# Block 1's front stage: TensorE's order written out by a plan of threads, and a row-by-row inverse

## The chip, the cores and the metric
One core of one Trainium2 chip runs the whole program; the metric is device microseconds of that core from one launch, as the median of several runs (the lower the better). TensorE (PE) is fed by VectorE (DVE), ScalarE (ACT), and by DMAs that are all issued from the queue of SyncE (SP).

## The reference, cut to what matters
A sequence of 512 tokens of width 1024 passes through two blocks of two layers each. Block 1, which the change touches, computes in each layer:

```
h = rmsnorm(x);  p = h @ w_in                 # 1792 + 1536 + 1024 + 3*1024 columns
y_rw  = rwkv7(p_rw)      # S_t = S_{t-1}(diag(w_t) - kk_t^T (a_t kk_t)) + v_t^T k_t ; y_t = S_t r_t, then group norm, gate
y_ret = retention(p_ret) # rotary, 4 heads, decayed causal scores, rms norm, silu gate
y_sg  = sgu(p_sg)        # gelu, layer norm, causal 128-token mixing
x = x + sum_n(sigmoid(gate_n) * (y_n @ w_branch_n)) @ w_out
x = x + conv_ffn(rmsnorm(x))
```

Block 2 (five attention branches, merge) follows; the change leaves its code alone.

## The kernel before, in words
Activations lie transposed, 128 channels by 512 tokens to a tile. A product with a weight is made of two rounded halves on each side (hi and lo): `mm3` (lines 110 to 112) issues three matmuls for each block of 128 by 128 weights. One `wraw` load of 512 KB holds eight such blocks; ScalarE rounds it to `whi` (L101) and VectorE takes the rest to `wlo` (L102). An output tile of 128 channels (`fm_tile`) is thus 24 matmuls of 512 columns into one PSUM bank of the pool `pm`, which VectorE empties (`evac`, L360, or `gate`, L783). `tm_group` makes a tile with tokens on the partitions, 4 x 24 matmuls of 256 columns. These are called dense work below.

A layer of block 1 has a front stage (everything up to the first `pbr` matmul), a merge (`pbr`, then `w_out`) and a feed-forward part. The front stage holds:

- `rwkv_in`: 14 dense tiles; after tiles 2 to 4, 5 to 7, 8 to 10, 11 to 13 one "pair" of heads is prepared (decays, normalised keys, `psA`). Its two sums over a head (`psk`, `psbon`) go through DRAM and back to be spread over the partitions (`sums`, L137: tiles `sums`, `sumd`, then the target).
- `rwkv_inverse`: 32 triangular 32x32 matrices at once on VectorE: for each of 31 rows one multiply (L487) and one reduction (L489).
- `rwkv_out`: 16 units (4 pairs x 4 chunks of 128 tokens) of small fp32 matmuls that depend on one another (`pst`, `psam`, `psv`, `psg`, `psh`, `psu`, `psy`, `psx`), two units side by side by `robin`, and for each pair `rw_final` (six `psz` steps in a row, `psY`, then a mean and a norm by the same way through DRAM: L642, L650, and the gate).
- `retention`, `sgu` and `gates`: a generator `fill` that `paced` advances by fixed rates (`PACE`) between the steps above. Of the 24 gate tiles 20 are made here and stored to DRAM, 4 are made during the merge (the tuple `e1`).

The order in which each engine gets its instructions is not the order of the code: a scheduler that simulates the engines picks it, by priorities; the code gives evacuations and weight halves a head start of 3000 places (`AHEAD`). Each engine then takes its instructions strictly in that order, so that one that waits holds all that stand behind it. PSUM's eight banks in block 1 are shared out as 3 `pm`, 3 `pw` (chains), 2 `pf` (retention, sgu).

Of the kernel before, what the change touches and what calls it, by code (L numbers as in the profile page):

```python
# [44 lines left out]
HALF = object()  # L45


class Kern:
    BANKS = dict(act=(3, 3, 2), act2=(3, 5, 0))
    AHEAD = 3000  # L50
    PACE = {"in": 0.55, "inv": 3.8, "out": 0.088}
    BUFS = dict(F=8, T=4, h=16, C4=3, Y=8, KR=4, K=4, B=4, V=4, R=2, E=2, WK=7, M=4)
# [258 lines left out]

    def tm_group(self, src, evac):

        ws = [self.weights(src[i], 1024) for i in range(2)]
        for g in range(4):
            ps = self.PM([128, 512])
            for k in range(KD):
                w = ws[k // 4]
# [4 lines left out]
        yield


    def block1_layer(self, l, next_gain, gain1=None, side=None):
# [7 lines left out]
        self.yret, self.ysg = [], []  # L334
        fill = itertools.chain(self.retention(l, win), self.sgu(l, win), self.gates(I["w_gt1"][l], 3, self.cfg.get("e1", (1, 3, 2, 3, 3, 3, 3, 2))))
        self.pump = lambda n: [next(fill, None) for _ in range(n)]
        self.due = 0.0
        self.rwkv_in(l, win)
        self.rwkv_inverse()
        self.paced("inv")  # L340
        yrw = self.rwkv_out(l)
        self.pump(1000)
        ys = [yrw, [self.split(y, *self.seat1(i)) for i, y in enumerate(self.yret)],
              [self.split(y, *self.seat1(4 + i)) for i, y in enumerate(self.ysg)]]
# [5 lines left out]
    def paced(self, part):  # L350

        self.due += self.cfg.get("pace", self.PACE)[part]
        while self.due >= 1:
            self.due -= 1
            self.pump(1)

    def evac(self, ps, tag, name="ev"):
        t = self.tile(tag, name=name)
        with self.tc.high_priority(offset=self.AHEAD):
            self.nc.vector.tensor_tensor(t, ps, self.rb, op=OP.mult)  # L360
        return t


    def rw_mix(self, i, ws, tag):
        nc = self.nc
        p = self.evac(self.fm_tile(ws), "E")
# [3 lines left out]
        self.paced("in")  # L370
        return m

    def rwkv_in(self, l, win):
# [19 lines left out]
        for f in range(4):
            fs = slice(f * 128, (f + 1) * 128)
            r = self.rw_mix(2 + 3 * f, ws, "R")
            k = self.rw_mix(3 + 3 * f, ws, "K")
            vt = self.rw_mix(4 + 3 * f, ws, "V")
            psw = self.P(name="psw")
            nc.tensor.matmul(psw, lhsT=lora[0:64, fs], rhs=m[0:64, :], start=True, stop=True)
            psa = self.P(name="psa")  # L400
            nc.tensor.matmul(psa, lhsT=lora[64:128, fs], rhs=m[64:128, :], start=True, stop=True)
            sw = W("sw")
            nc.scalar.activation(sw, psw, AF.Tanh, bias=half[:, f:f + 1], scale=0.5)
            nc.vector.tensor_scalar(sw, sw, 0.5, 0.5, op0=OP.mult, op1=OP.add)
            a = W("a")
            nc.scalar.activation(a, psa, AF.Tanh, bias=half[:, 4 + f:5 + f], scale=0.5)

            sq = W("sqk")
            nc.scalar.activation(sq, k, AF.Square, scale=v(V_KK + f))

            def inverse(t, ps):
                nc.vector.tensor_scalar(t, ps, 1e-24, None, op0=OP.max)
                nc.scalar.activation(t, t, AF.Sqrt)
                nc.vector.reciprocal(t, t)
            self.sums(sq, self.sel[:, 0], 2, self.P([128, 128], "psk"), sq, inverse)
            kkr = self.tile("B", name="kkr")
# [2 lines left out]
            sc = W("sc")
            nc.vector.tensor_tensor_scan(sc, self.reset, sw, initial=0.0, op0=OP.mult, op1=OP.add)  # L420
            s3 = sc.rearrange("p (c t) -> p c t", t=64)
            dd = self.ap.tile([128, 24], F32, name="dd", tag="dd", bufs=2)
            mid = dd[:, 8:16]
            nc.vector.tensor_copy(mid, s3[:, :, 31])
            nc.vector.tensor_tensor(dd[:, 0:7], s3[:, 0:7, 63], mid[:, 0:7], op=OP.subtract)
            nc.vector.tensor_tensor(dd[:, 0:7], dd[:, 0:7], mid[:, 1:8], op=OP.add)
            nc.scalar.activation(dd[:, 0:7], dd[:, 0:7], AF.Exp, scale=-KAPPA)
            ds = self.ap.tile([128, 8], F32, name="ds", tag="ds", bufs=4)
            nc.sync.dma_start(ds[64:128, 0:7], dd[0:64, 0:7])
            nc.sync.dma_start(ds[0:64, 0:7], dd[64:128, 0:7])  # L430
            self.DD.append(ds)
            nc.vector.tensor_tensor(s3, s3, mid.unsqueeze(2).to_broadcast([128, 8, 64]), op=OP.subtract)
            e1 = W("e1")
            nc.scalar.activation(e1, sc, AF.Exp, scale=-KAPPA)
            nc.vector.tensor_tensor(sw, sc, sw, op=OP.subtract)
            e0 = sw
            nc.scalar.activation(e0, e0, AF.Exp, scale=-KAPPA)
            ei = sc
            nc.scalar.activation(ei, sc, AF.Exp, scale=KAPPA)
            kr = self.tile("KR", (128, 4, 2, 128), name="kr")  # L440
            g4 = lambda t: t.rearrange("p (g t) -> p g t", g=4)
            nc.vector.tensor_tensor(kr[:, :, 0, :], g4(kkr), g4(e0), op=OP.mult)
            nc.vector.tensor_tensor(kr[:, :, 1, :], g4(r), g4(e1), op=OP.mult)
            bd = kkr
            nc.vector.scalar_tensor_tensor(bd, a, 1.0, kkr, op0=OP.add, op1=OP.mult)
            nc.vector.scalar_tensor_tensor(bd, bd, 0.5, ei, op0=OP.mult, op1=OP.mult)

            for e in range(2):
                ps = self.P([128, 4, 64], "psA")
                hs = slice(64 * e, 64 * e + 64)  # L450
                for g in range(4):
                    for c in range(2):
                        cs = slice(64 * c, 64 * c + 64)
                        nc.tensor.matmul(ps[cs, g, :], lhsT=bd[hs, g * 128 + 64 * c:g * 128 + 64 * c + 64],
                                         rhs=kr[hs, g, 0, cs], start=True, stop=True, skip_group_check=True)
                u0 = f * 8 + e * 4
                for b in range(4):
                    bs, ts = slice(32 * b, 32 * b + 32), slice(32 * (b % 2), 32 * (b % 2) + 32)
                    nc.scalar.activation(self.CP[bs, :, u0:u0 + 4].rearrange("p t u -> p u t"), ps[bs, :, ts], AF.Copy)

            nc.vector.tensor_scalar(a, a, -1.0, half[:, 8 + f:9 + f], op0=OP.add, op1=OP.mult)
            nc.vector.scalar_tensor_tensor(k, a, 1.0, k, op0=OP.add, op1=OP.mult)
            nc.vector.scalar_tensor_tensor(r, r, v(V_RK + f), k, op0=OP.mult, op1=OP.mult)
            kd = k
            nc.vector.tensor_tensor(kd, k, ei, op=OP.mult)
            bv = W("bv")
            self.sums(r, self.sel[:, 0], 2, self.P([128, 128], "psbon"), bv,
                      lambda t, ps: nc.scalar.activation(t, ps, AF.Copy))
# [1476 lines left out]
```

## Time and profile before

| | us |
|---|---|
| median of 3 runs (3474.56 to 3478.92) | 3475.21 |
| the profiled execution | 3473.58 |
| its span, first to last instruction | 3471.9 |
| front stage, layer 0: 21.5 to 562.9 | 541.4 |
| merge up to the last `pbr`, layer 0: to 651.8 | 88.9 |
| front stage, layer 1: 1068.7 to 1606.6 | 537.9 |
| merge up to the last `pbr`, layer 1: to 1695.4 | 88.8 |

A front stage is taken from the end of the norm that comes ahead of it (`psb`) to the first `pbr` matmul. In the profile a row's "busy" is the time in which the engine had an instruction in hand; matmuls overlap, so the pace of TensorE is the distance from one start to the next. The granted clock is a share of 2.4 GHz.

### The profile page before, as it was taken

How to read it: one execution, taken by the hardware profiler on the slowest of the kernel's cores; microseconds unless marked ns; L12 is line 12 of the kernel's file. 1: busy time of each engine (PE TensorE's matmuls, PEld its weight loads, DVE VectorE, ACT ScalarE, POOL GpSimd, SP SyncE). 2: the span in 40 equal slices, each digit the busy share in tenths (PEclk: the TensorE clock that was granted, in tenths of full speed). 3: DMA queues.
4: the chain of work that ended last, by engine and by line, in shares of the span. 5: the costliest groups of instructions: out<-in, count | busy, mean ns of one | idle time of the engine just before them, and what ended most of it. 6: DMA issues, size and time to landing. Idle time of an engine off the chain costs nothing.

```text
span 3471.9 us, 47315 instructions
## 1 busy us (share of the span) xinstructions
PE 3332.2 (96%) x17944; PEld 2633.0 (76%) x17944; DVE 2239.1 (64%) x4112; ACT 1346.2 (39%) x2392; POOL 116.2 (3%) x137
## 2 busy tenths in 40 slices
PE   8888999999999989999999999899999999999998
PEld 6667767888887667777888888786778887777776
DVE  5577554687634567564677635797766659866665
ACT  4343223344424433223444434335334443443342
POOL 0000000000000000000000000001001200000031
PEclk9999999999999989999999999999999999999999
DMA  4332224433333331224533335544436554543463
GB/s 137 90 93 62 65 72 155 162 115 97 121 116 99 94 90 52 76 68 153 166 101 95 121 127 156 174 148 124 128 113 230 195 152 135 149 127 120 136 216 137
DMA packets 197940, 431.21 MB, mean 124 GB/s; under 512 B 29512, under 2 KB 57544, under 8 KB 197712
## 3 DMA queue, kind: packets, MB, share of 16 engines
q1 hardware_dynamic: 197712, 428.18, 39.9%
q8 instruction: 142, 2.33, 0.3%
q14 instruction: 86, 0.70, 0.1%
HBM read 337.47 MB, written 59.39 MB: 114 GB/s over the span
## 4 chain that ended last, share of the span: by engine, by line
PE 80%; DMA 9%; DVE 7%; ACT 2%; issue 2%; SPq 1%; POOL 0%; DVEq 0%; ACTq 0%; POOLq 0%
PE pm L112 20%; PE pm L110 19%; PE pm L111 19%; PE pbr L110 2%; PE pbr L112 2%; PE pbr L111 2%; PE psy L1028 2%; DMA sqr<-sumd 2%; PE pspt L1018 2%; DVE wlo L102 1%; DMA sumd<-sums 1%; DMA cc<-sumd 1%; DMA bv<-sumd 1%; DMA sqk<-sumd 1%; PE psl L1000 1%
## 5 line engine op out<-in xcount | busy, mean ns | idle before, releaser
L110 PE MATMUL pm<-shi,whi 128*128 128x512 f32 x3072 | 1230.5, 401 | 10.9 <-ACT whi L101 10.8
L112 PE MATMUL pm<-shi,wlo 128*128 128x512 f32 x3072 | 1221.9, 398 | 3.3 <-DVE wlo L102 3.0
L111 PE MATMUL pm<-slo,whi 128*128 128x512 f32 x3072 | 1221.4, 398 | 0.0
L101 ACT ACTIVATE whi<-wraw 128x1024 fp32r<-128x1024 f32 x480 | 508.5, 1059 | 988.5 <-PE pm L111 671.9
L102 DVE TENSOR_TENSOR wlo<-wraw,whi 128x1024 fp32r<-128x1024 f32 x480 | 588.8, 1227 | 215.6 <-ACT whi L101 208.1
L110 PEld LDWEIGHTS pm<-shi,whi 128*128 128x128 f32 x3072 | 581.7, 189 | 146.1 <-ACT whi L101 16.0
L112 PEld LDWEIGHTS pm<-shi,wlo 128*128 128x128 f32 x3072 | 581.7, 189 | 139.1 <-DVE wlo L102 10.3
L111 PEld LDWEIGHTS pm<-slo,whi 128*128 128x128 f32 x3072 | 582.5, 190 | 125.5 <-issue 10.4
L783 DVE TENSOR_TENSOR gate<-pm,rb 128x512 f32<-128x512 f32 x128 | 88.2, 689 | 196.5 <-PE pm L112 195.9
L360 DVE TENSOR_TENSOR ev<-pm,rb 128x512 f32<-128x512 f32 x140 | 96.2, 688 | 119.1 <-PE pm L112 117.3
L110 PE MATMUL pm<-whi,shi 128*128 128x256 f32 x384 | 115.8, 303 | 3.4 <-ACT whi L101 2.0
L111 PE MATMUL pm<-wlo,shi 128*128 128x256 f32 x384 | 116.0, 302 | 1.5 <-DVE wlo L102 1.4
L112 PE MATMUL pm<-whi,slo 128*128 128x256 f32 x384 | 115.6, 302 | 0.0
L110 PE MATMUL pbr<-shi,whi 128*128 128x512 f32 x288 | 114.2, 397 | 1.4 <-DVE gate L815 1.2
L112 PE MATMUL pbr<-shi,wlo 128*128 128x512 f32 x288 | 113.5, 394 | 0.4 <-DVE wlo L102 0.4
L111 PE MATMUL pbr<-slo,whi 128*128 128x512 f32 x288 | 113.0, 392 | 0.0
L815 DVE SCALAR_TENSOR_TENSOR gate<-gate,pbr 128x512 f32<-128x512 f32 x128 | 85.8, 683 | 33.2 <-PE pbr L112 29.0
L819 POOL TENSOR_TENSOR gate<-gate 128x512 f32<-128x512 f32 x48 | 77.5, 1614 | 606.5 <-DVE gate L815 342.9
L812 ACT ACTIVATE gate<-gate 128x512 f32<-128x512 f32 x128 | 76.4, 624 | 29.4 <-DMA gate<-gtd 28.6
L985 ACT ACTIVATE p<-psl,st 128x256 f32<-128x256 f32 (+3 forms) x128 | 65.1, 513 | 52.2 <-DVE st L983 44.4
L110 PEld LDWEIGHTS pm<-whi,shi 128*128 128x128 f32 x384 | 78.5, 205 | 8.9 <-issue 4.0
L111 PEld LDWEIGHTS pm<-wlo,shi 128*128 128x128 f32 x384 | 78.8, 205 | 8.3 <-issue 5.3
(478 smaller groups left out, 4507.5 us busy)
## 6 DMA issues: line engine op xcount, KB each, us to landing
wraw<-in_w_gt SPq DMA_DIRECT2D x148, 512.0 KB, 3.6
wraw<-in_w_in SPq DMA_DIRECT2D x116, 512.0 KB, 3.7
wraw<-in_f_up SPq DMA_DIRECT2D x88, 512.0 KB, 3.5
gtd<-gate SPq DMA_DIRECT2D x108, 256.0 KB, 2.0
gate<-gtd SPq DMA_DIRECT2D x108, 256.0 KB, 4.1
wraw<-in_w_br SPq DMA_DIRECT2D x44, 512.0 KB, 3.5
wraw<-in_f_dn SPq DMA_DIRECT2D x44, 512.0 KB, 3.5
wraw<-in_w_out SPq DMA_DIRECT2D x32, 512.0 KB, 3.5
```

Of the source, the lines that this page charges most:

```text
L101: nc.scalar.activation(hi[:, :n], raw[:, :n], AF.Copy)
L102: nc.vector.tensor_tensor(lo[:, :n], raw[:, :n], hi[:, :n].bitcast(F32), op=OP.subtract)
L110: nc.tensor.matmul(ps, lhsT=lhs[0], rhs=rhs[0], start=first, stop=False, skip_group_check=skip)
L111: nc.tensor.matmul(ps, lhsT=lhs[0], rhs=rhs[1], start=False, stop=False, skip_group_check=skip)
L112: nc.tensor.matmul(ps, lhsT=lhs[1], rhs=rhs[0], start=False, stop=last, skip_group_check=skip)
L360: self.nc.vector.tensor_tensor(t, ps, self.rb, op=OP.mult)
L783: self.nc.vector.tensor_tensor(t, ps, self.rb, op=OP.mult)
L812: nc.scalar.activation(g, g, AF.Tanh, scale=0.5)
L815: nc.vector.scalar_tensor_tensor(g, g, 1.0, pb, op0=OP.add, op1=OP.mult)
L819: (nc.gpsimd if self.pre and n in self.cfg.get("pa", (1, 2, 3)) else nc.vector).tensor_tensor(g, g, acc, op=OP.add)
L1018: nc.tensor.transpose(pt_[:, b * 128:(b + 1) * 128], ps[e][:, b * 128:(b + 1) * 128], self.ident)
L1028: nc.tensor.matmul(psy[64 * e:64 * e + 64, :], lhsT=vs[e][b], rhs=pts[e][:, b * 128:(b + 1) * 128], start=first and b == 0, stop=last and ...
```

## The change: what it does
The front stage of block 1 is written as generators that yield `Step(cost, wait, chain, inner)`, and a `Plan` walks them: it keeps a time `t` of TensorE's work, takes every chain step that is due, and otherwise a dense piece of the thread of lowest rank (`rwkv_in` 1, retention and sgu 2, gates 3). A dense tile is cut in pieces of two weight blocks (`MORE`), between which due chain steps go; a tile that is begun is finished before another. The plan runs under `manual_schedule(engines={PE})`: TensorE gets its instructions in the order in which the plan traced them; the other engines are ordered by the scheduler as before.

With it come: pairs, units (two lanes), finals, retention's ends as chain threads with declared waits; `late()`, by which a VectorE operation that waits for a DMA is queued behind the evacuation traced last; all 24 gates made in the front stage; the branches in the merge in the order retention, sgu, rwkv (`ORDER1`, with the weights laid out to match); banks 2/4/2; the inverse column by column (outer products: multiply and add of (31-s) x (s+1) elements, s from 1 to 30); v in a zero-padded tile `vp`, copied by ScalarE, so that the second `psy` matmul covers 128 columns; `zs` folded into `cc`; the last gate's `psg` copied by ScalarE.

```diff
+class Plan:
+    def step(self, th):
+        s = next(th["gen"], None)
...
+        self.t += s.cost
+        th["chain"], th["due"] = s.chain, self.t + s.wait
...
+    def run(self):
+        while self.threads:
+            due = sorted((th for th in self.threads if th["chain"] and th["due"] <= self.t), key=lambda th: th["due"])
+            for th in due:
+                self.step(th)
+            dense = [th for th in self.threads if not th["chain"] and th["due"] <= self.t]
+            if self.held:
+                self.step(self.held)
+            elif dense:
+                self.step(min(dense, key=lambda th: th["rank"]))
+            elif self.threads and not due:
+                t = min(th["due"] for th in self.threads)
+                self.lost += max(t - self.t, 0.0)
+                self.t = max(t, self.t)
...
-    BANKS = dict(act=(3, 3, 2), act2=(3, 5, 0))
+    BANKS = dict(act=(2, 4, 2), act2=(3, 5, 0))
...
+        with self.tc.manual_schedule(engines={mybir.EngineType.PE}):
+            plan.add(self.rwkv_in(l, win), 1)
+            plan.add(self.branches(l, win), 2)
+            plan.add(self.gates1(I["w_gt1"][l], 3, (3,) * KD), 3)
+            plan.run()
...
+    def late(self):
+        return self.tc.issue_after(self.last.ins)
...
+        self.sums(sq, self.sel[:, 0], 2, self.P([128, 128], "psk"), sq, inverse)
...
+        yield Chain(0.4, 13.0)
+        kkr = self.tile("B", name="kkr")
+        with self.late():
             nc.vector.scalar_tensor_tensor(kkr, k, v(V_KK + f), sq, op0=OP.mult, op1=OP.mult)
...
-        for t in range(1, 32):
-            nc.vector.tensor_tensor(tmp[:, 0:t, 0:t], R[:, 0:t, 0:t].rearrange("p s c -> p c s"),
-                                    X[:, t, None, 0:t].to_broadcast([128, t, t]), op=OP.mult)
-            nc.vector.tensor_reduce(R[:, t, 0:t], tmp[:, 0:t, 0:t], axis=AX.X, op=OP.add)
+        nc.vector.tensor_copy(R[:, 1:32, 0:1], X[:, 1:32, 0:1])
+        for s in range(1, 31):
+            n, m = 31 - s, s + 1
+            nc.vector.tensor_tensor(tmp[:, 0:n, 0:m], X[:, s + 1:32, s:s + 1].to_broadcast([128, n, m]),
+                                    R[:, s, None, 0:m].to_broadcast([128, n, m]), op=OP.mult)
+            nc.vector.tensor_tensor(R[:, s + 1:32, 0:m], R[:, s + 1:32, 0:m], tmp[:, 0:n, 0:m], op=OP.add)
...
+        vp = self.vp[lane]
+        nc.scalar.activation(vp[:, 0:4:3, :], pst[:, 3, :].rearrange("p (e v) -> p e v", e=2), AF.Copy)
...
-            nc.tensor.matmul(psy[vs, e, :], lhsT=tk[:, 2, vs], rhs=ams[e][:, 384:512],
-                             start=False, stop=True, skip_group_check=True)
+            nc.tensor.matmul(psy[:, e, :], lhsT=vp[:, 2 * e:2 * e + 2, :].rearrange("p a v -> p (a v)"),
+                             rhs=ams[e][:, 384:512], start=False, stop=True)
...
-        yield
-        nc.vector.tensor_tensor(y0, y0, mean, op=OP.add)
-        yield
+        yield Chain(0.4, 10.0)
+        with self.late():
+            nc.vector.tensor_tensor(y0, y0, mean, op=OP.add)
```

## Rows read from the trace of the kernel before

**Rows 1.** The page's head and part 1: span; busy us (share) and instructions.
```profile
span 3471.9 us, 47315 instructions
PE 3332.2 (96%) x17944; PEld 2633.0 (76%) x17944; DVE 2239.1 (64%) x4112; ACT 1346.2 (39%) x2392; POOL 116.2 (3%) x137
```

**Rows 2.** Windows: us, busy (instructions) of each engine, granted clock, DMA share, GB/s.
```profile
21.50:562.90 541.40, 491.96 (x3152) 371.96 (x3151) 324.34 (x596) 182.59 (x374) 0.64 (x1) 0.94 0.28 83
562.90:651.80 88.90, 88.90 (x385) 72.13 (x384) 52.71 (x66) 35.97 (x48) 0.00 (x0) 1.00 0.49 157
1068.70:1606.60 537.90, 495.54 (x3173) 375.51 (x3172) 324.74 (x592) 182.24 (x374) 0.64 (x1) 0.95 0.28 84
...
2650.40:2740.60 90.20, 89.29 (x385) 71.65 (x384) 61.66 (x76) 39.16 (x57) 36.92 (x23) 1.00 0.56 184
```

**Rows 3.** Windows inside layer 0's front stage.
```profile
100.00:200.00 100.00, 83.80 (x444) 59.08 (x443) 58.60 (x94) 43.65 (x69) 0.00 (x0) 0.91 0.34 89
200.00:300.00 100.00, 85.86 (x485) 66.68 (x484) 73.40 (x126) 31.22 (x54) 0.64 (x1) 0.88 0.30 78
```

**Rows 4.** Windows of the instructions on tile pm alone, both front stages.
```profile
21.50:562.90 541.40, 342.04 (x1443) 250.73 (x1443) 30.88 (x45) 7.32 (x16) 0.94 0.28 83
1068.70:1606.60 537.90, 344.41 (x1463) 253.19 (x1463) 30.99 (x45) 7.29 (x16) 0.95 0.28 84
```

**Rows 5.** Timeline of TensorE: start, us, line, operation; dense matmuls at full clock.
```profile
555.20 0.39 PE L112 MATMUL pm<-shi,wlo 128*128 128x512 f32 x1
...
562.68 0.39 PE L112 MATMUL pm<-shi,wlo 128*128 128x512 f32 x1
```

**Rows 6.** Timeline of TensorE: psu, psy and psx of one unit.
```profile
309.09 0.72 PE L575 MATMUL psu<-rhs,tt 128*128 128x128 f32 x5
309.65 0.39 PE L753 MATMUL pssg<-wst,vsg 128*128 128x128 f32 x2
309.88 0.46 PE L583 MATMUL psy<-am,uw 128*128 128x128 f32 x2
310.26 0.43 PE L585 MATMUL psy<-am,tk 128*64 128x128 f32 x2
...
311.40 0.33 PE L600 MATMUL psx<-tk,uw 64*64 64x64 f32 x2
```

**Rows 7.** VectorE's waits in layer 0's front stage: us, times, longest.
```profile
DVE yret L714 <- DMA sqr<-sumd: 21.7, 4, 7.5
DVE y L642 <- DMA cc<-sumd: 20.0, 4, 6.9
DVE bv L469 <- DMA bv<-sumd: 15.6, 4, 5.4
DVE kkr L417 <- DMA sqk<-sumd: 13.1, 3, 5.6
```

**Rows 8.** Timelines of VectorE and TensorE around one such wait.
```profile
146.27 0.69 DVE L714 TENSOR_TENSOR yret<-yret,sqr 128x512 f32<-128x512 f32 x1 [7.48 <-DMA sqr<-sumd]
147.49 1.65 PE L707 MATMUL psret<-pret,vret 128*128 128x384 f32 x2 [5.49 <-DVE pret L706]
```

**Rows 9.** The inverse in layer 0's front stage, by lines: busy us, mean ns.
```profile
L487 DVE TENSOR_TENSOR tmp<-R,X 128x1 f32<-128x1 f32 (+30 forms) x31 | 23.5, 757 | 0.5
L489 DVE TENSOR_REDUCE R<-tmp 128x1 f32<-128x1 f32 (+30 forms) x31 | 15.3, 494 | 0.4
```

**Rows 10.** The chain that ended last: a way through DRAM, and two ends of pairs.
```profile
60.71 0.87 DVE sums L414
...
64.36 6.30 DMA sqk<-sumd
...
351.32 0.96 PE psY L633 x28
...
410.12 0.96 PE psY L633 x28
```

**Rows 11.** Timeline of VectorE in the merge: emptying a pbr bank.
```profile
588.00 0.69 DVE L815 SCALAR_TENSOR_TENSOR gate<-gate,pbr 128x512 f32<-128x512 f32 x1 [0.67 <-PE pbr L112]
```

More of the change, by code (lines that the diff above doesn't have):

```diff
@@ L45, with __init__, Chain, Dense @@
 HALF = object()
+LANES = 2
+class Step:
+    def __init__(self, cost, wait=0.0, chain=False, inner=False):
+        self.cost, self.wait, self.chain, self.inner = cost, wait, chain, inner
+def Chain(cost, wait):
+    return Step(cost, wait, chain=True)
+def Dense(cost):
+    return Step(cost)
+MORE = Step(1.4, inner=True)
+TILE = Dense(1.4)
+class Plan:
+    def __init__(self):
+        self.t, self.threads, self.held, self.lost = 0.0, [], None, 0.0
+    def add(self, gen, rank, wait=0.0):
+        self.threads.append(dict(gen=gen, rank=rank, chain=rank == 0, due=self.t + wait))
+    def step(self, th):
+        s = next(th["gen"], None)
+        if s is None:
+            self.threads.remove(th)
+            self.held = None if self.held is th else self.held
+            return
+        self.t += s.cost
+        th["chain"], th["due"] = s.chain, self.t + s.wait
+        if s.inner:
+            self.held = th
+        elif self.held is th:
+            self.held = None
+    def run(self):
[12 more added lines that the diff above has]
+                self.t = max(t, self.t)
 class Kern:
-    BANKS = dict(act=(3, 3, 2), act2=(3, 5, 0))
+    BANKS = dict(act=(2, 4, 2), act2=(3, 5, 0))
     AHEAD = 3000
-    PACE = {"in": 0.55, "inv": 3.8, "out": 0.088}
-    BUFS = dict(F=8, T=4, h=16, C4=3, Y=8, KR=4, K=4, B=4, V=4, R=2, E=2, WK=7, M=4)
+    BUFS = dict(F=8, T=4, h=16, C4=3, Y=8, KR=4, K=4, B=4, V=4, R=2, E=2, WK=8, M=3)
     BUFS2 = dict(A=23, ix=1, V=6, p=6, pt=4, sw=2, Y=4, c=2, cum=2)
@@ L310, in fm_tile, with fm_steps @@
         return ps
+    def fm_steps(self, ws):
+        ps = self.PM(name="pm")
+        for k in range(KD):
+            self.mm3(ps, next(ws), self.h[k], k == 0, k == KD - 1)
+            if k % 2 and k < KD - 1:
+                yield MORE
+        return ps
     def tm_group(self, src, evac):
@@ L332, in block1_layer @@
         win = I["w_in1"]
[L334 to L344, printed above, removed]
+        self.yret, self.ysg, self.yrw = [], [], [None] * 4
+        plan = self.plan = Plan()
+        with self.tc.manual_schedule(engines={mybir.EngineType.PE}):
[3 more added lines that the diff above has]
+            plan.run()
+        ys = [[self.split(y, *self.seat1(i)) for i, y in enumerate(self.yret)],
+              [self.split(y, *self.seat1(4 + i)) for i, y in enumerate(self.ysg)], self.yrw]
         self.merge(l, ys, I["w_br1"], I["w_out1"], lambda c: self.v(V_N2 + c),
@@ L348, in block1_layer, with branches @@
         self.ffn(l, next_gain, gain1, side)
[L350 to L355, printed above, removed]
+    def branches(self, l, win):
+        yield from self.retention(l, win)
+        yield from self.sgu(l, win)
     def evac(self, ps, tag, name="ev"):
@@ L359, in evac @@
         with self.tc.high_priority(offset=self.AHEAD):
-            self.nc.vector.tensor_tensor(t, ps, self.rb, op=OP.mult)
+            self.last = self.nc.vector.tensor_tensor(t, ps, self.rb, op=OP.mult)
         return t
+    def late(self):
+        return self.tc.issue_after(self.last.ins)
     def rw_mix(self, i, ws, tag):
         nc = self.nc
-        p = self.evac(self.fm_tile(ws), "E")
+        p = self.evac((yield from self.fm_steps(ws)), "E")
         m = self.tile(tag, name="mix")
@@ L391, in rwkv_in @@
         self.CP = self.tile("C4", (128, 32, 32), name="CP")
-        W = lambda name: self.tile("WK", name=name)
[L393 to L416, printed above, removed]
-            nc.vector.scalar_tensor_tensor(kkr, k, v(V_KK + f), sq, op0=OP.mult, op1=OP.mult)
[L419 to L468, printed above, removed]
-            nc.vector.tensor_tensor(bv, bv, vt, op=OP.mult)
-            bvd = self.dp.tile([128, S], F32, name="bvd", tag="bvd", bufs=4)
-            nc.sync.dma_start(bvd, bv)
-            self.KR.append(kr); self.BD.append(bd); self.KD_.append(kd); self.VF.append(vt); self.BV.append(bvd)
@@ L497, in rwkv_out, with lane, rw_unit @@
         self.gup = gup
-        self.yrw = [None] * 4
-        last = None
-        for f in range(4):
-            st = dict((n, self.tile("WK", (128, 8, 64), name=n)) for n in ("y0", "rdw", "xt", "cc"))
-            for g in (0, 2):
-                run = [self.rw_unit(f, g, st), self.rw_unit(f, g + 1, st)]
-                if g == 0 and last:
-                    run.append(last)
-                for _ in robin(run):
-                    self.paced("out")
-            last = self.rw_final(l, f, st)
-        for _ in robin([last]):
-            self.paced("out")
-        return self.yrw
-    def rw_unit(self, f, g, st):
+        self.units = [(f, g) for f in range(4) for g in range(4)]
+        self.states, self.left, self.ended = {}, [4] * 4, [False] * 4
+        for i in range(LANES):
+            self.plan.add(self.lane(l, i), 0, 2.0 * i)
+    def lane(self, l, i):
+        while self.units:
+            f, g = self.units[0]
+            if f > 1 and not self.ended[f - 2]:
+                yield Chain(0.0, 1.0)
+                continue
+            self.units.pop(0)
+            if g == 0:
+                self.states[f] = dict((n, self.tile("WK", (128, 8, 64), name=n)) for n in ("y0", "rdw", "xt", "cc"))
+            yield from self.rw_unit(f, g, self.states[f], i)
+            self.left[f] -= 1
+            if not self.left[f]:
+                self.plan.add(self.rw_final(l, f, self.states[f]), 0, 2.0)
+    def rw_unit(self, f, g, st, lane):
         nc = self.nc
@@ L521, in rw_unit @@
         u0 = f * 8 + g
-        small = lambda shape, name, bufs=2: self.ap.tile(shape, F32, name=name, tag=name, bufs=bufs)
+        small = lambda shape, name: self.ap.tile(shape, F32, name=name, tag=name, bufs=LANES)
         pst = self.P([128, 4, 128], "pst")
@@ L538, in rw_unit @@
         ttf = tt.rearrange("p u b t -> p u (b t)")
-        yield
-        am = self.am[g % 2]
+        yield Chain(0.6, 1.0)
+        am = self.am[lane]
         ams = [am[:, e].rearrange("p m t -> p (m t)") for e in range(2)]
+        psa = [self.P([128, 4, 64], "psam") for _ in range(2)]
         for e in range(2):
             hs = slice(64 * e, 64 * e + 64)
-            psa = self.P([128, 4, 64], "psam")
             for m, t in enumerate((bd, kd)):
@@ L603, in rw_unit @@
                                  skip_group_check=True)
-                nc.tensor.matmul(psx[os, 1, :], lhsT=tk[cs, 1, us], rhs=tk[cs, 2, us], start=False, stop=True,
+                nc.tensor.matmul(psx[os, 1, :], lhsT=tk[cs, 1, us], rhs=vp[cs, 3 * e, :], start=False, stop=True,
                                  skip_group_check=True)
@@ L648, in rw_final @@
         nc.sync.dma_start(bv, self.BV[f])
-        yield
-        nc.vector.tensor_tensor(y0, y0, sq, op=OP.mult)
+        psg = self.P(name="psgate")
+        nc.tensor.matmul(psg, lhsT=self.gup[:, f * 128:(f + 1) * 128], rhs=self.sgd, start=True, stop=True)
+        gt = mean
+        nc.scalar.activation(gt, psg, AF.Copy)
+        yield Chain(1.6, 11.0)
+        with self.late():
+            nc.vector.tensor_tensor(y0, y0, sq, op=OP.mult)
         nc.vector.tensor_scalar(y0, y0, v(V_LG + f), v(V_LB + f), op0=OP.mult, op1=OP.add)
         nc.vector.tensor_tensor(y0, y0, bv, op=OP.add)
-        psg = self.P(name="psgate")
-        nc.tensor.matmul(psg, lhsT=self.gup[:, f * 128:(f + 1) * 128], rhs=self.sgd, start=True, stop=True)
-        nc.vector.tensor_tensor(y0, psg, y0, op=OP.mult)
+        nc.vector.tensor_tensor(y0, gt, y0, op=OP.mult)
         self.dump("yrw%d_%d" % (l, f), y0)
         self.yrw[f] = self.split(y0, "KR")
-        yield
+        self.ended[f] = True
+        yield Chain(0.0, 0.0)
     def seat1(self, i):
@@ L673, in retention @@
             for i in range(2):
[L674 to L675 removed]
+                t = self.evac((yield from self.fm_steps(ws)), "F")
                 sw = T(name="swp")
@@ L712, in retention, with ret_end @@
                 nc.vector.scalar_tensor_tensor(y, psy, 0.5, gt, op0=OP.mult, op1=OP.mult)
+                yield Chain(0.4, 3.0)
                 self.norms(sq, self.sel[:, 1], 1, self.PF([128, 128], "psrn"), bias=self.eps[:, 0:1], scale=1.0 / 128)
-                nc.vector.tensor_tensor(y, y, sq, op=OP.mult)
-                self.dump("yret%d_%d" % (l, h), y)
-                self.yret.append(y)
+                self.plan.add(self.ret_end(l, h, y, sq), 0, 12.0)
+                yield Dense(0.4)
+    def ret_end(self, l, h, y, sq):
+        with self.late():
+            self.nc.vector.tensor_tensor(y, y, sq, op=OP.mult)
+        self.dump("yret%d_%d" % (l, h), y)
+        self.yret.append(y)
+        yield Chain(0.0, 0.0)
     def sgu(self, l, win):
@@ L726, in sgu @@
                                 channel_multiplier=-1)
-        ps = self.PF([128, 4, 128], "pswsum")
-        nc.tensor.matmul(ps, lhsT=self.ones, rhs=wst, start=True, stop=True)
-        for gr in range(4):
-            nc.vector.scalar_tensor_tensor(bs[:, gr], ps[:, gr], self.v(V_SB + gr), bs[:, gr], op0=OP.mult, op1=OP.add)
         vt = [F(name="vsg") for _ in range(4)]
@@ L736, in sgu @@
             yield from self.tm_group([win[l, 26 + 2 * hf], win[l, 27 + 2 * hf]], ev)
+        ps = self.PF([128, 4, 128], "pswsum")
+        nc.tensor.matmul(ps, lhsT=self.ones, rhs=wst, start=True, stop=True)
+        for gr in range(4):
+            nc.vector.scalar_tensor_tensor(bs[:, gr], ps[:, gr], self.v(V_SB + gr), bs[:, gr], op0=OP.mult, op1=OP.add)
         st = self.ap.tile([128, 4, 6], F32, name="bst", tag="bst", bufs=1)
@@ L745, in sgu @@
             nc.vector.tensor_scalar(vt[g], vt[g], ag[:, g, 0:1], ag[:, g, 3:4], op0=OP.subtract, op1=OP.mult)
+        yield Dense(1.1)
         ws = self.stream(win[l, 30:34])
         for gr in range(4):
-            u = self.evac(self.fm_tile(ws), "F")
-            yield
+            u = self.evac((yield from self.fm_steps(ws)), "F")
             nc.scalar.activation(u, u, AF.Gelu)
+            yield Chain(0.0, 3.5)
             ps = self.PF([128, 4, 128], "pssg")
@@ L760, in sgu @@
             self.ysg.append(y)
+            yield Dense(0.9)
     def silus(self, wgt, n):
@@ L784, in gate, with gate_streams, gate_out, gates @@
         return t
-    def gates(self, wgt, nb, early):
+    def gate_streams(self, wgt, nb, early):
         self.gd = {}
         self.gs = self.stream([wgt[nb * c + n] for c in range(KD) for n in range(early[c], nb)])
-        ws = self.stream([wgt[nb * c + n] for c in range(KD) for n in range(early[c])])
+        return self.stream([wgt[nb * c + n] for c in range(KD) for n in range(early[c])])
+    def gate_out(self, c, n, g):
+        d = self.dp.tile([128, S], F32, name="gtd", tag="gtd", bufs=50)
+        self.nc.sync.dma_start(d, g)
+        self.gd[c, n] = d
+    def gates(self, wgt, nb, early):
+        ws = self.gate_streams(wgt, nb, early)
         for c in range(KD):
             for n in range(early[c]):
-                g = self.gate(ws, "T")
-                d = self.dp.tile([128, S], F32, name="gtd", tag="gtd", bufs=50)
-                self.nc.sync.dma_start(d, g)
-                self.gd[c, n] = d
+                self.gate_out(c, n, self.gate(ws, "T"))
                 yield
+    def gates1(self, wgt, nb, early):
+        ws = self.gate_streams(wgt, nb, early)
+        for c in range(KD):
+            for n in range(early[c]):
+                self.gate_out(c, n, self.evac((yield from self.fm_steps(ws)), "T", "gate"))
+                yield TILE
     def merge(self, l, ys, wbr, wout, gain, stag=None, split=True):
@@ L1656, in run @@
                     self.am = [self.ap.tile([128, 2, 4, 128], F32, name="am%d" % i) for i in range(2)]
+                    self.vp = [self.ap.tile([128, 4, 64], F32, name="vp%d" % i) for i in range(2)]
                     for t in self.am:
                         nc.gpsimd.memset(t.rearrange("p e m t -> p (e m t)"), 0.0)
+                    for t in self.vp:
+                        nc.gpsimd.memset(t.rearrange("p a v -> p (a v)"), 0.0)
                     for l in range(L1):
```

151 lines of the change are left out of this document (118 added, 33 removed).

## Prediction
> **What bounds the kernel now.** I read the page first: TensorE is busy 96% of the span, the vector engine 64% [rows 1], so TensorE sets the time, and the question is what its busy time holds. Then windows by stage. The merge runs at full clock without a gap (88.90 busy of 88.90), the front stages of block 1 don't: 491.96 of 541.40 us in layer 0, 495.54 of 537.90 in layer 1, at a granted clock of 0.94 and 0.95 [rows 2]. So 49.4 and 42.4 us are idle. Cutting the stage up shows where: 16.2 us in 100 to 200 and 14.1 in 200 to 300, 30 of the 49, at clocks of 0.91 and 0.88 [rows 3], the stretch of the pairs, the retention and the inverse.
>
> The idle time is only part of the loss, since a matmul in hand at half clock counts as busy. Dense matmuls at full clock start 0.2267 us apart: 33 steps from 555.20 to 562.68 [rows 5]. Layer 0's 1443 rows on `pm` are 1059 of 512 columns and 384 of 256 (half the pace): 1059 x 0.2267 + 384 x 0.1133 = 283.6 us, against 342.0 busy, 58.4 over [rows 4]. About 71 times a chain step cuts in behind a dense matmul, whose row then runs 0.39 - 0.23 = 0.16 us past the pace [rows 5]: 11 us that are no loss. Layer 1: 1079 x 0.2267 + 43.5 = 288.1, against 344.4, 56.3 over. The loss is 49.4 + 58.4 - 11 = 97 us in layer 0 and 42.4 + 56.3 - 11 = 88 in layer 1, 185 together. A lower count takes the clock by itself: 0.06 x 541.4 + 0.05 x 537.9 = 59 and the idle 92 make 151. The first compares like with like, so I take 185 and keep 151 as a bound.
>
> What makes it: the vector engine takes its instructions in a fixed order, and four kinds of them wait for a way through DRAM: `yret` 21.7, `y` 20.0, `bv` 15.6, `kkr` 13.1 us, 70 us in layer 0 [rows 7]. One such wait in full: up to 146.27 it stood 7.48 us before `yret`, with the product for `psret` behind it; TensorE sat idle 5.49 of these until 147.49 [rows 8]. Dense tiles need the vector engine too (`wlo`, bank emptying), so they are no cover while it is held.
>
> **The change, part by part.**
>
> *Order and `late()`.* The four operations are queued behind the last evacuation and come 10 to 13 us after the sums were issued. A way through DRAM took 60.71 to 70.66, 10 us, from the reciprocal on [rows 10]; so most land in time, and what is behind them isn't held. Dense pieces stand between chain steps in TensorE's own order. The upper end is the whole 185 us; the lower end is below zero, since a fixed order can stall too (rival 2). What stays, per layer: (a) the 14 tiles of `rwkv_in` now stand back to back, with three pairs' vector work beside 76 us, where before it was spread to 214 us; over the whole stage the vector engine was 60% busy (324 of 541 [rows 2]), in this part it will be near full: 10 us. (b) By the code some 204 chain steps per layer (16 pairs', 112 units', 36 finals', 36 retention's, 4 sgu's), each at a place fixed by a declared wait; with 0.07 us lost on the mean, 15 us. (c) The start, the end and what clock these cost: 8 us. 33 per layer, an estimate between 10 (only the idle 5% that TensorE shows where no way through DRAM comes) and 80 (as now); gain 185 - 66 = 119.
>
> *`psy`.* Now 309.88 to 311.40, 1.52 us a unit, as the array changes between 128*128 and 128*64; `psu`, the same matmuls in one shape, takes 0.56 / 5 = 0.112 a row [rows 6], so eight rows become 0.90. 0.62 x 32 units = 20 us gained, on TensorE, which is the path. The ends: 0 (if the excess were waiting) and 25.
>
> A chain step set alone between dense pieces changes the array's shape twice. The Trainium skill, TensorEngine Tiling (Array Packing), Key Properties, says that a change of tiling mode drains TensorE, which speaks against finer interleaving. The `psy` rows agree that changes cost (0.62 us for four, 0.16 each [rows 6]). By the code I count 208 changes per layer after (64 units', 72 finals', 32 pairs', 40 retention's), all of which exist before too unless two units stood side by side; if a third were new, that would be 70 x 0.16 = 11 us per layer, 22 together, and the sum 22 us worse.
>
> *Gates.* Four tiles per layer move from the merge to the front, 4 x 24 x 0.2267 = 21.8 us each way: zero. In exchange the merge loads 24 gates and not 20; its DMA goes from 157 to about (24 x 0.26 + 12 x 0.52) MB / 67 us = 190 GB/s, and block 2's merge takes 184 with TensorE busy 89.29 of 90.20 [rows 2]. If the cover failed, 0.9 us per merge.
>
> *Banks 2/4/2.* A `pbr` tile is 12 matmuls, 2.7 us; with two banks one must be emptied within that. It took 0.69 us, and the vector engine was waiting for it [rows 11]. Zero; a bank late by 1 us at each of 24 tiles would be 24 us per merge.
>
> *The inverse.* 23.5 + 15.3 = 38.8 us of vector work in 62 instructions [rows 9]; after, 60 of 5425 elements twice over, some 17 us at 1 ns an element and 0.1 us each. 21 us of vector time and of the chain; nothing by itself, as the chain isn't last: `rwkv_in` ends near 21.5 + 66 + 9 = 97, the last pair 31 later, the inverse 26, eight rounds of two units at the pace of now, (410.12 - 351.32) / 2 = 29 us [rows 10], the last final 45: 431. TensorE's own work lasts to 21.5 + 541.4 - 97 - 10 + 21.8 + 33 = 511. So 80 us of slack; the smaller vector work only makes (a) smaller. Below nothing, if the scheduler put it ahead of `wlo` as one block: 17 us, hidden in the idle of rival 1.
>
> *ScalarE's new copies* (`vp`, `gt`): under 0.5 us each, 20 per layer, on an engine busy 183 of 541 us [rows 2]; zero.
>
> **Sum.** Against the profiled execution's 3473.6 (span 3471.9 and 1.7 around it; the median is 1.6 above it): -119 - 20 = 3334.6, and 1 us for the median: **3335**.
>
> **Rivals.**
> 1. *Chains become the bound.* In-order TensorE, two lanes only, a vector engine near full in the first 150 us: if a round of two units takes 40 and not 29 us and the pairs end 25 us late, the chain ends at 431 + 88 + 25 = 544, 33 past 511. Gain 139 - 66 = 73: 3402. For it: a unit has seven steps in a row, each over two engines; against: the 80 us of slack.
> 2. *The fixed order stalls: slower.* Before, the scheduler's order let dense work pass a late chain; afterwards a late operand holds all of TensorE. Place: the 204 steps; price: the mean lateness beyond the declared wait; it decides from (185 + 20) / 408 = 0.5 us a step. At 0.63, 257 - 205 = +52: 3526. For it: the waits are constants, and the ways through DRAM vary; the vector engine waited for `yret` up to 7.5 us [rows 7]. Against: most declared waits are 2 to 4 us for operations of 0.2 to 0.7.
> 3. *Everything is hidden*: 10 us per layer stay: 185 - 20 + 20 = 185: 3290 or a little under.
> 4. *It doesn't do what it says.* `late()` pins only against the evacuation traced last; the next ones may stand behind the waiting operation as before. Then 70 us per layer of holds [rows 7] stay in the vector engine and only a third of the loss goes: 62 + 20 at the most: 3392 to 3470.
>
> **How the numbers follow.** The forecast (3290 to 3385) 0.58; rival 1, 0.15; rival 2, 0.09; rival 3, 0.12; rival 4, 0.06, a third of it within the 0.2% (7 us) that is about what a measurement can tell from no change. Faster 0.89, same 0.02, slower 0.09. The range of 8 in 10 leaves out rivals 2 and 4 and the tail of 3: 3275 to 3425.
>
> **What would show it.** Right: front stages of about 489 and 495 us to the first `pbr` and merges of 67; clock above 0.97 between 100 and 300; the four waits for DRAM in the vector engine's list under 20 us; `psy` at 0.112 us a row; the `pbr` rows unbroken. Wrong: TensorE idle before `psam`, `psA`, `psret` with the vector engine busy (rival 1), or waiting on declared steps all through 150 to 450 (rival 2); holds before `kkr` and `y` as now (rival 4); gaps between `pbr` tiles (the banks or the gate loads).

## The result and the profile after

The changed kernel took 3335.82 us (median of 4 runs, 3334.16 to 3336.96), the kernel before beside it 3477.07 (3474.56 to 3478.92): a ratio of 0.9594 (95% interval 0.9577 to 0.961), 141 us less; the forecast was 3335. (The "row-by-row inverse" of the title is the old one: the change makes it column by column.) The page's head and part 1 after (busy us, share, instructions):

```profile
span 3335.3 us, 47337 instructions
PE 3245.5 (97%) x17944; PEld 2596.1 (78%) x17944; DVE 2194.4 (66%) x4062; ACT 1365.3 (41%) x2440; POOL 116.7 (3%) x139
```

TensorE issues the same 17944 instructions in 87 us less busy time [rows 1]. The stages, cut as before [rows 2]: the two front stages and the merges behind them, then block 2's first layer from its norm to its first `pbr` (columns: us, busy (instructions) of PE, PEld, DVE, ACT, POOL, granted clock, DMA share, GB/s):

```profile
21.00:499.30 478.30, 467.69 (x3264) 370.20 (x3263) 306.68 (x574) 197.39 (x404) 0.84 (x1) 0.99 0.34 105
499.30:572.90 73.60, 68.96 (x290) 55.39 (x289) 48.27 (x63) 29.69 (x40) 0.00 (x0) 0.98 0.55 169
990.20:1473.10 482.90, 469.25 (x3269) 371.52 (x3267) 306.62 (x570) 197.60 (x405) 0.63 (x1) 0.99 0.34 103
1473.10:1548.00 74.90, 69.91 (x290) 56.07 (x289) 48.21 (x63) 29.81 (x40) 0.00 (x0) 0.95 0.54 166
...
1968.80:2512.80 544.00, 526.86 (x2981) 415.78 (x2981) 389.29 (x936) 218.02 (x467) 14.02 (x35) 0.99 0.51 150
```

Before, the last of these was this row:

```profile
2117.50:2650.40 532.90, 517.56 (x2944) 408.09 (x2943) 388.86 (x937) 217.58 (x469) 14.10 (x35) 0.99 0.51 152
```

| stage | before | after | |
|---|---|---|---|
| front, layers 0 and 1 | 541.4, 537.9 | 478.3, 482.9 | -63.1, -55.0 |
| merge, layers 0 and 1 | 88.9, 88.8 | 73.6, 74.9 | -15.3, -13.9 |
| block 2, norm to first `pbr` | 532.9 | 544.0 | +11.1 |
| all the rest | | | -0.4 |
| span | 3471.9 | 3335.3 | -136.6 |

The front holds four more gate tiles and is still shorter. In layer 0 its idle time went from 49.4 to 478.30 - 467.69 = 10.6 us, the clock from 0.94 to 0.99. The weak stretch [rows 3] and the vector engine's waits for DRAM [rows 7] show the same thing, first windows, then waits (us, times, longest):

```profile
100.00:200.00 100.00, 94.10 (x533) 71.18 (x532) 78.46 (x154) 39.04 (x70) 0.00 (x0) 0.97 0.40 123
200.00:300.00 100.00, 99.82 (x801) 80.75 (x800) 54.17 (x110) 35.83 (x92) 0.00 (x0) 1.00 0.29 81
```

```profile
DVE kkr L523 <- DMA sqk<-sumd: 7.1, 3, 5.2
DVE y L739 <- DMA cc<-sumd: 6.0, 2, 4.5
DVE yret L822 <- DMA sqr<-sumd: 5.4, 1, 5.4
```

In 200 to 300 TensorE starts 801 matmuls where it started 485, and the waits for DRAM fell from 70.4 to 18.5 us (19.9 in layer 1; the `bv` wait is gone; a fifth, before the last step of `y`, stayed at 4.8 for 4.0).

The merge shows what the forecast lacked. The chain of waits, then TensorE's timeline, where the first `pbr` of the `rwkv` branch stands:

```profile
502.10 2.36 DMA sumd<-sums
...
505.15 6.31 DMA rdw<-sumd
511.55 0.70 DVE y L752
...
514.31 0.64 ACT shl L181
515.02 0.77 PE pbr L168
```

```profile
515.02 0.77 PE L168 MATMUL pbr<-shi,whi 128*128 128x512 f32 x1 [4.64 <-ACT shl L181]
```

The last pair's norm is still on its way through DRAM when the front's dense work ends at 499.3; the retention and sgu branches, which now come first, cover it but for 4.64 us (5.0 in layer 1). The rest of what the merges took beyond the 67 us forecast goes with a granted clock of 0.98 and 0.95 where it was 1.00.

### The profile page after: what moved, and what is told of

Its sections match the earlier page's. It is cut to its first block, busy times and chain, and to the rows that moved or that the text cites. A ratio compares the mean times of both kernels' runs of the same rounds, so it can differ in the third digit from the quotient of the medians.

```text
span 3335.3 us, 47337 instructions
## 1 busy us (share of the span) xinstructions
PE 3245.5 (97%) x17944; PEld 2596.1 (78%) x17944; DVE 2194.4 (66%) x4062; ACT 1365.3 (41%) x2440; POOL 116.7 (3%) x139
## 4 chain that ended last, share of the span: by engine, by line
PE 85%; DVE 6%; DMA 5%; ACT 2%; issue 1%; SPq 1%; POOL 0%; DVEq 0%; ACTq 0%; POOLq 0%
PE pm L168 22%; PE pm L170 21%; PE pm L169 21%; PE psy L1152 2%; PE pbr L168 2%; PE pbr L169 2%; PE pbr L170 2%; PE pspt L1142 2%; DVE wlo L160 2%; PE psl L1124 1%; DMA rdw<-sumd 1%; PE psl L1125 1%; DMA sqr<-sumd 1%; PE pssc L804 1%; DMA zd<-z 1%
## 5 line engine op out<-in xcount | busy, mean ns | idle before, releaser
L894 DVE TENSOR_TENSOR gate<-pm,rb 128x512 f32<-128x512 f32 x80 | 55.1, 689 | 121.6 <-PE pm L170 121.3
```

## The experiments

Medians; each ratio is against runs of the kernel before on the same chip (medians 3474.47 to 3477). "After" stands for the changed kernel.

**Without `late()`** (in the changed kernel).
```diff
-        return self.tc.issue_after(self.last.ins)
+        return nullcontext()
```


> The changed kernel (3336 us) with late() an empty context: the four VectorE operations that wait for a way through DRAM may again stand ahead of evacuations and weight halves. Theory of the prediction (the holds of VectorE make the loss): most of the 50 us of holds per layer that went come back, and TensorE stalls behind them: 3400 to 3430. Rival (the plan's places and waits alone do it, the operations are traced 10 to 13 us later anyway): VectorE's waits for DRAM stay near 20 us per layer and the time within 10 us of 3336.


3374.87 us, 0.9708 (0.9693 to 0.9722): 39 more than after. The fronts lasted 498.7 and 500.1 us. The vector engine's waits in the first (21 to 519.7):

```profile
DVE yret L822 <- DMA sqr<-sumd: 22.7, 4, 8.3
DVE kkr L523 <- DMA sqk<-sumd: 17.9, 4, 5.9
DVE sqk L552 <- DMA sqk<-sumd: 12.1, 4, 6.3
DVE y L739 <- DMA cc<-sumd: 2.4, 2, 1.5
```

Three of the four waits are back (55.1 us in all, for 18.5), and the front is 20.4 us longer: in this run a us more of the vector engine's waits went with about half a us of front. `y` stayed short without the pin (2.4 for 6.0), so for it the plan's place is enough here.

**TensorE's order left to the scheduler.**
```diff
-        with self.tc.manual_schedule(engines={mybir.EngineType.PE}):
+        with nullcontext():
```


> The changed kernel with TensorE's order left to the scheduler (the plan still sets the order of tracing, late() stays). Theory of the prediction: the order is the smaller part, 20 to 40 us lost: 3356 to 3376, VectorE's waits for DRAM stay short. Rival (the fixed order is the main thing, the scheduler starts chain steps too early and dense work too late): 90 us or more lost, 3426 and up.


3334.11 us (3328.73 to 3338.05), 0.9586 (0.9566 to 0.9606): no difference from after, though the two orders differ. So pinning TensorE's order neither gains nor stalls anything that can be measured here. What stays of the plan is the order in which it traces; that the scheduler's priorities come from it is an inference, as no run undid the tracing order alone.

**The narrow `psy` matmul.**
```diff
-            nc.tensor.matmul(psy[:, e, :], lhsT=vp[:, 2 * e:2 * e + 2, :].rearrange("p a v -> p (a v)"),
+            nc.tensor.matmul(psy[vs, e, :], lhsT=vp[:, 3 * e, :],
```


> The changed kernel with the second psy matmul back at 64 columns in its own half of the partitions (array shapes 128*128 and 128*64 in turn). Theory: psy goes from 0.112 back to about 0.19 us a row, 0.5 to 0.6 us for each of 32 units, all of it on TensorE's path: 16 to 20 us, 3352 to 3356. Rival (the excess was waiting that other work would fill): under 5 us.


3350.22 us, 0.9636 (0.9621 to 0.965): 14.4 more, 0.45 us for each of 32 units, where the forecast had 0.62. Windows of `psy` alone in layer 0's front, before, then after:

```profile
21.50:562.90 541.40, 25.66 (x128) 15.72 (x128) 9.06 (x32) 8.64 (x32) 0.94 0.28 83
```
```profile
21.00:499.30 478.30, 17.30 (x128) 15.79 (x128) 9.21 (x32) 8.64 (x32) 0.99 0.34 105
```

The same 128 rows take 8.4 us less; with the narrow form put back they take 24.86 in either layer:

```profile
21.40:508.60 487.20, 24.86 (x128) 15.93 (x128) 9.24 (x32) 8.66 (x32) 0.99 0.34 103
```

Counted in the traces, the array's shape changes 246 times a front in this run and 198 times after, 48 more, three a unit: 14.4 us for 96 changes, 0.15 us each. The fourth change of a unit, into `psx`, is there in both. The Trainium skill's rule that a change of tiling mode drains TensorE (TensorEngine Tiling (Array Packing), Key Properties) agrees; it gives no price.

**The inverse row by row, as before** (the old loop put back), and **that with the order left to the scheduler too**.
```diff
+        for t in range(1, 32):
+            nc.vector.tensor_tensor(tmp[:, 0:t, 0:t], ...
+            nc.vector.tensor_reduce(R[:, t, 0:t], tmp[:, 0:t, 0:t], axis=AX.X, op=OP.add)
```


> The changed kernel with the row-by-row inverse back (38.8 us of VectorE a layer against some 17). Theory of the prediction, that the chain is not last (80 us of slack): 0 to 5 us. Rival, from the trace after, where the last pair's final ends at 514 and the merge waits for it: TensorE's order is fixed with 26 us allowed for the inverse, so psg waits some 15 to 20 us per layer for it: 3366 to 3376.

> The row-by-row inverse of the earlier run (3372 us with TensorE's order fixed), with TensorE's order left to the scheduler. Theory (a fixed order makes TensorE wait for the late inverse): the scheduler fills the time, 3336 to 3350. Rival (the chain behind the inverse sets the end of the front, whoever orders TensorE): 3365 to 3380.


3372.37 us (3367.39 to 3380.86), 0.9701 (0.9679 to 0.9723): 36.5 more. With the free order 3360.1 (3357.29 to 3364.64), 0.9674 (0.9659 to 0.9688): 24 more than after. The first kernel's windows in layer 0, then the second's:

```profile
100.00:200.00 100.00, 88.53 (x493) 65.55 (x491) 82.33 (x138) 37.09 (x64) 0.00 (x0) 0.94 0.40 121
200.00:300.00 100.00, 93.95 (x684) 75.90 (x684) 57.46 (x108) 29.47 (x77) 0.00 (x0) 0.93 0.22 65
```
```profile
100.00:200.00 100.00, 94.10 (x523) 70.34 (x522) 85.51 (x143) 39.02 (x69) 0.00 (x0) 0.97 0.40 122
200.00:300.00 100.00, 94.35 (x757) 75.86 (x756) 60.70 (x118) 32.12 (x87) 0.00 (x0) 0.95 0.25 72
```

The vector engine is 82 to 86% busy in 100 to 200 (78% after), and in the first kernel the first `psg` comes at 216.9 and not 198.2 and the stage ends 18.5 us later. "Nothing by itself" was wrong. What TensorE waits for there (186 to 217), and the vector engine's timeline meanwhile:

```profile
PE psret L807 <- DVE pret L805: 6.6, 2, 5.9
PE psam L645 <- ACT rhs L629: 5.0, 1, 5.0
```
```profile
193.84 1.49 DVE L576 TENSOR_TENSOR tmp<-R,X 128x784 f32<-128x784 f32 x1
195.23 0.43 DVE L624 COPY tk<-pst 128x256 f32<-128x256 f32 x1
...
206.34 1.14 DVE L578 TENSOR_REDUCE R<-tmp 128x31 f32<-128x961 f32 x1
...
209.58 1.05 DVE L631 TENSOR_TENSOR tt<-T,c_bmask 128x256 f32<-128x256 f32 x2
...
211.11 0.42 DVE L805 TENSOR_TENSOR pret<-pssc,dec 128x256 f32<-128x256 f32 x1
```

In that stretch TensorE waits 11.6 us for `pret` and for a ScalarE copy behind `tk`, both of which stand behind rows of the inverse in the vector engine's queue, and not for the inverse at `psg`, as the recorded rival had it; the granted clock there (200 to 250) is 0.85 for 1.00. With the free order `psg` itself waits 4.0 us for `tt`, which is made from the inverse. The free order's time is 12 us shorter, but the intervals of the ratios overlap, so a share of the pinned order isn't shown.

**Banks 3/3/2.**
```diff
-    BANKS = dict(act=(2, 4, 2), act2=(3, 5, 0))
+    BANKS = dict(act=(3, 3, 2), act2=(3, 5, 0))
```


> The changed kernel with the PSUM banks back at 3 pm, 3 pw, 2 pf. Question: why block 2's first layer, whose code is the same, starts 10 us later after its norm than before (37 dense matmuls ran ahead of psb before, none after). Theory: block 2's third pm bank is the first pw bank of block 1 when block 1 has only two pm banks, so its dense work waits for the norm; with 3/3/2 the 8 to 10 us come back, and the units lose a little to the third pw bank: 3326 to 3336. Rival (the banks have no part in it, and pw is short in the units): block 2's start stays late and the time is 3340 or more.


3359.98 us (3354.73 to 3366.22), 0.9666 (0.9649 to 0.9682): 24 more. The fronts, and block 2's stage:

```profile
21.10:511.90 490.80, 472.22 (x3266) 372.66 (x3264) 307.33 (x574) 197.83 (x404) 0.83 (x1) 0.99 0.33 102
...
1000.80:1500.30 499.50, 475.86 (x3267) 374.95 (x3267) 307.45 (x570) 197.91 (x405) 0.85 (x1) 0.98 0.33 100
...
1992.80:2529.40 536.60, 519.74 (x2943) 409.78 (x2942) 389.00 (x937) 218.61 (x469) 13.95 (x35) 0.98 0.50 152
```

Moving the bank from dense tiles to the chains is worth 12.5 and 16.6 us of front; against that block 2's stage gets back 7.4 of its 11 us.

**PSUM's pools laid out `pm`, `pf`, `pw`.** What had happened in block 2, in TensorE's timeline after:

```profile
1956.71 0.40 PE L170 MATMUL pm<-shi,wlo 128*128 128x512 f32 x1
1960.67 2.34 PE L331 MATMUL psn<-ones,sq 128*128 128x1 f32 x16 [3.57 <-DVE sq L302]
1965.42 3.66 PE L192 MATMUL psb<-c_ident,rcol 128*128 128x128 f32 x16 [2.41 <-DVE rcol L340]
1970.08 0.46 PE L168 MATMUL pm<-shi,whi 128*128 128x512 f32 x1 [1.00 <-DVE rb L346]
```

No dense matmul stands between the norm's steps. By the code the pools lie one behind the other, so with 2/4/2 block 2's third `pm` bank is one that block 1 used for its chains. The edit:
```diff
-        k.pm, k.pw, k.pf = [...for t, n in zip(("pm", "pw", "pf"), k.BANKS[name])...]
+        k.pm, k.pf, k.pw = [...for t in ("pm", "pf", "pw")]
```


> The changed kernel with the same 2/4/2 banks, laid out pm, pf, pw instead of pm, pw, pf, so that block 2's third pm bank is one of retention's. Theory (block 2's first dense work waits for a chain bank that the norm uses): dense matmuls run ahead of psb again and 6 to 10 us come back, 3326 to 3330. Rival (the late start comes from the order of loads): no change, 3334 to 3338.


3328.1 us (3327.76 to 3328.76), 0.9581 (0.9566 to 0.9595): 8 less than after by the times, though the ratios' intervals overlap. Its trace, timeline and stage window:

```profile
1959.40 0.95 PE L331 MATMUL psn<-ones,sq 128*128 128x1 f32 x8
1960.21 0.49 PE L168 MATMUL pm<-shi,whi 128*128 128x512 f32 x1
...
1960.76 0.95 PE L331 MATMUL psn<-ones,sq 128*128 128x1 f32 x8
```
```profile
1968.80:2504.60 535.80, 518.97 (x2944) 409.36 (x2943) 388.77 (x937) 217.16 (x468) 14.01 (x35) 0.98 0.51 152
```

Dense matmuls run between the norm's steps again, and the stage takes 8.2 us less.

**Two gate tiles back in the merge.**
```diff
-            plan.add(self.gates1(I["w_gt1"][l], 3, (3,) * KD), 3)
+            plan.add(self.gates1(I["w_gt1"][l], 3, (1,) + (3,) * (KD - 1)), 3)
```


> The changed kernel with two gate tiles per layer (row 0, branches 2 and 3) left to the merge. Theory: the merge's first rwkv matmul waits 7 to 9 us for the last final; two gate tiles, 10.9 us of dense work, cover that, and the front is 10.9 us shorter if TensorE and not the chain sets its end: 6 to 8 us per layer gained, 3320 to 3324. Rival (the last chain sets the end of the front too): the front doesn't get shorter, the merge gets longer by what it computes, 3336 to 3350.


3323.07 us, 0.9561 (0.9547 to 0.9575): 13 less. Front and merge of layer 0:

```profile
21.10:487.00 465.90, 455.77 (x3208) 360.70 (x3207) 301.77 (x568) 190.28 (x394) 0.87 (x1) 0.99 0.33 100
487.00:567.70 80.70, 79.61 (x347) 63.45 (x346) 53.08 (x69) 36.90 (x50) 0.00 (x0) 1.00 0.61 187
```

The front ends 12.4 us earlier and the merge takes 7.1 more, with 1.1 us idle for 4.6: the two tiles fill the wait for the last pair. So it is dense work and not the chain that ends the front. **Both together:**


> The layout pm, pf, pw together with two gates per layer left to the merge. If the two gains add: 3323 less 6 to 10, so 3313 to 3317. If the bank theory is wrong: 3321 to 3325.


3313.61 us (3308.61 to 3315.35), 0.9536 (0.9522 to 0.9551): the two gains add, and this version beats both kernels.

**Parts put into the kernel before:** the column inverse alone (the loop of the change), and `late()` alone, on its five operations.
```diff
+            with self.late():
+                nc.vector.scalar_tensor_tensor(kkr, k, v(V_KK + f), sq, op0=OP.mult, op1=OP.mult)
```


> The kernel before with the column-by-column inverse alone. Theory of the prediction (vector work beside a path that TensorE sets): within 8 us of before, 3469 to 3477. Rival, from the row-inverse run of the changed kernel, where it was worth 36 us: the 21 us per layer are on the path before too: 3430 to 3445.

> The kernel before with late() on the five operations that wait for a way through DRAM (kkr, bv, both of the final, yret), and nothing else. If the rule of queueing alone ends the holds: 30 to 60 us gained, 3415 to 3445. Rival (in this code they are traced right behind their sums, so the evacuation traced last already stands ahead of them; only the plan's later place makes the rule bite): within 8 us of before.


The inverse: 3456.09 us, 0.9943 (0.9926 to 0.9959), 20.6 less, a small gain but clear of the noise. `late()`: 3476.42 (3470.86 to 3479.88), 1.0 (0.9991 to 1.0009), nothing. Its vector engine still waits:

```profile
DVE yret L723 <- DMA sqr<-sumd: 20.7, 4, 7.0
DVE y L649 <- DMA cc<-sumd: 19.1, 4, 6.6
DVE bv L475 <- DMA bv<-sumd: 15.4, 4, 5.0
DVE kkr L422 <- DMA sqk<-sumd: 13.3, 3, 5.5
```

So in the old code rival 4 is what happens: the pin stands behind an evacuation, but not late enough. That it works where the plan traces the operation steps later fits this run and the 39 us above; no run moved the place alone.

**The plan alone:** no `late()`, the row inverse, the narrow `psy` (the three edits above together).


> The changed kernel with three parts undone together: late() empty, the row-by-row inverse, psy at 64 columns. What is left is the plan's order, the four pw banks and the shorter finals. Undone singly they cost 39, 36 and 14 us. If they add: 3336 + 89 = 3425, and the rest is worth 52 of the 141 us. Rival (they hide one another, since all three lengthen the same chain): the loss is well under 89, 3380 to 3400; or the fixed order multiplies lateness: 3450 and up.


3404.13 us (3403.4 to 3407.2), 0.9801 (0.9785 to 0.9817): 68 more than after, not 39 + 36 + 14 = 89; the parts hide one another in some measure, and the time lies between the forecast sum and the rival's 3380 to 3400. What is left of the 141, some 73 us, is the plan's tracing order with the fourth chain bank, the shorter finals, the units' new forms and smaller edits, which weren't told apart.

## Why the prediction was right, and where it was not

**The loss in dense work: right in size.** On tile `pm` of layer 0's front after:

```profile
21.00:499.30 478.30, 347.69 (x1556) 262.63 (x1556) 34.23 (x50) 7.52 (x16) 0.99 0.34 105
```

With the same 384 rows of 256 columns, 1172 x 0.2267 + 43.5 = 309.2 us at pace [rows 4, 5], so 38.5 over; with 10.6 idle and less the same 11 for cut-ins, 38 us of loss stay, where the forecast had 33. Of 97 us 59 went (64 forecast). In layer 1, by the same sum, 42 stay: 46 of 88 went (55 forecast). The 71 cut-ins of the forecast are 138 in the trace (114 after); but the dense rows overlap the chain step behind them by 12.8 us before and after, so the 11 was near.

**What took it away: half right.** The forecast gave all of it to the order and `late()`. The waits for DRAM did go (18.5 and 19.9 us, under 20 as said), and `late()` is worth 39 us within the plan, but nothing alone, and the pinned order gives nothing. The fourth chain bank (12.5 to 16.6 a layer) and the inverse (36 us, or 20.6 in the old code) do part of that work. The step that failed is "nothing by itself, as the chain isn't last": the chain that was called 80 us early ended at 514 and not at 431. Every term of it was short: the last pair ends at 142 (128 forecast), the inverse takes 44 us from there (26), the eight rounds 268 (232, 34 us apart and not 29), the last final 60 (45). And the end of the chain was the wrong thing to ask: dense work ends the front (two gate tiles less, 12.4 us less), and yet the row-by-row inverse costs, with TensorE's order pinned through other operations that wait behind it on the vector engine. Its rows after, in the first layer:

```profile
L580 DVE TENSOR_TENSOR R<-R,tmp 128x60 f32<-128x60 f32 (+15 forms) x30 | 10.4, 347 | 0.8
L578 DVE TENSOR_TENSOR tmp<-X,R 128x60 f32<-128x60 f32 (+15 forms) x30 | 10.3, 343 | 0.8
```

That is 20.7 us where the forecast had some 17; 18 us of vector work less, not 21 [rows 9].

**`psy`: right in kind, a quarter too large**: 14.4 by its undoing for 20. The forecast took all four changes of a unit away, and the one into `psx` stays: from the first `psy` to `psx` a unit takes 0.98 to 1.09 us, where 0.90 was forecast. Not in the sum: `psam` and `psx`, whose two heads' matmuls of a unit now stand together. `psam` alone, before, then after:

```profile
21.50:562.90 541.40, 20.83 (x256) 14.26 (x256) 26.95 (x64) 0.94 0.28 83
```
```profile
21.00:499.30 478.30, 12.71 (x256) 8.65 (x256) 26.91 (x64) 0.99 0.34 105
```

It is 8.1 us less in busy time, and `psx` went from 21.46 to 17.13; the array's shape changes 198 times in this front where it changed 292 times. By the distances of starts I put this at some 10 us a layer, an estimate. The 46 changes that aren't of `psy` make 7 us of it at 0.15; the rest isn't explained. By the same measure the other small matmuls took some 12 us a layer less, which no term stood for either; part of that may be the higher clock. The forecast's worry that finer interleaving would add changes was wrong in sign.

**Gates and merge: the terms held, a wait was missed.** 67 us became 73.6 and 74.9, mostly since the last pair's way through DRAM ends behind the front (4.64 and 5.0 us idle). The `pbr` rows of the branches themselves are unbroken, as the two banks' zero said.

**Block 2: missed**, 11 us, of which the pools' layout gives back 8.

So the sum met the time because errors cancelled, which is luck: about 20 us of `psam` and `psx` and 24 of other small matmuls not forecast, against 14 too much forecast in the dense loss, 14 in the merges and 11 in block 2. Fronts of 478.3 and 482.9 stand beside 489 and 495 forecast. Rival 1 came about in part: the chain ended 15 us behind the front, but a round took 34 us and not 40, and what that cost is the wait in the merge. Rival 2 did not occur; rival 4 was right of `late()` in the old code only.

## What to carry to other kernels

Where an engine takes its instructions in order, a wait of 5 to 8 us in its queue is paid in part by whoever is fed through it; see that what it waits for is issued long before the code traces the waiting operation, since a pin alone moved nothing here. A chain with computed slack may still set the pace through the banks and the engine that it shares: undo each such part by itself before it is priced at zero. When PSUM is shared out anew, look at the next stage's first norm, and keep some dense work back for the last chain's tail.

## What was not expected of the hardware

A change of the array's shape cost 0.15 us (14.4 us for 96). Where two heads' small matmuls of one shape were put side by side, 256 `psam` rows went from 20.83 to 12.71 us. The granted clock was lower where TensorE had more gaps: 0.88 where TensorE was 86% busy [rows 3], 0.93 at 93.95 (the row inverse) and 1.00 at 99.82 in the same stretch.
